# Planned landing times of GpSimd's small loads in an encoder trunk whose instruction order is planned

## The chip, the core and the metric

The kernel runs on one core of one Trainium2 chip. The metric is the device time of one execution in microseconds (us). TensorE does the matrix products (the profile calls it PE, and its weight loads PEld), VectorE (DVE) and ScalarE (ACT) prepare operands and evaluate results, GpSimd (POOL) does small vector work and issues a part of the DMA transfers, and SyncE (SP) issues the rest. Each engine works through its own instructions strictly in the order in which they stand in its queue; semaphores order the engines against each other.

## What is computed

Two layers of a macaron encoder on 256 tokens of width 1024, in float32:

```
for l in range(2):
    x = LN(alpha*x + 0.5*swiglu(x, ffn_w_in[l,0], ffn_w_out[l,0]))   # D_FF = 2816
    y = mlstm(x) if l == 0 else window_attention(x)
    x = LN(alpha*x + y)
    x = LN(alpha*x + 0.5*swiglu(x, ffn_w_in[l,1], ffn_w_out[l,1]))
```

The mLSTM projects x to q, k, v (4 heads), an output gate, and 16 gate columns (input and forget gates of both directions). From the gates it forms per head and direction a running sum and a running maximum over the tokens; the weights `exp(u - max)` multiply the products q k, and the result multiplies v.

## The kernel before

**How the work is tiled.** The weights stream from HBM in words of 128 x 1024 numbers (512 KB, one DMA each). A word is split into two float32r parts: ACT casts it to `w_hi`, DVE subtracts to get `w_lo`, and PE multiplies three times (hi by hi, hi by lo, lo by hi) with moving operands 512 wide. There are ten buffers for `w_hi` and ten for `w_lo`, so ACT and DVE can run ten words ahead of PE; raw words and other tiles of that size share sixteen buffers called "big". The feed-forward layers use a seven-product scheme for blocks of 512 columns (products P1, P2, S1 to S4, A22), in which some words are sums of two blocks: either DVE adds them, or POOL issues a DMA that adds a block from HBM onto the word in place (tiles `b11`, `b12`, `b22`). Between the products stand transposes of the finished activations (T0, T1) and one word each of the second matrix (`d`). `h_hi` and `h_lo` are the split transposed activations; their PSUM bank is free again when DVE has written `h_lo`.

**What sets the order.** The kernel body does not issue instructions. Each call is noted as a `Step` with its operands in a `Book`, and the order is planned afterwards. `latest` (line 392) gives each step a due time: PE's steps follow each other in program order, and every other step is due its own duration (and the delay until its result is seen) before the earliest step that needs it. `sequence` (line 420) then plays the engines against modelled durations: at each point it takes the step that can start first, and among those that can start the one that is due first; PE keeps program order. The steps are emitted in the order that comes out (line 596, which is therefore the line of nearly every instruction in the profile), and a step's buffer is chosen on the way. So a number in the model does not act on the chip by itself; it moves instructions within the queues of DVE, ACT, POOL and SP, and it can change which buffer a tile gets.

**The small loads.** A constant tile `few` of 128 x 192 holds small things that POOL loads with its own DMAs (`small_loads`, line 723, noted at the end of the first feed-forward stage): `gw`, the 16 gate columns of the mLSTM's input matrix (64 KB in runs of 64 bytes, since each of the 1024 matrix rows gives 16 numbers), four pieces of four gate biases (after a memset), the norm gains, and the attention sinks, which POOL then negates. ACT casts the gate columns to the float32r tile that is also named `gw` (after POOL has cleared it), and DVE writes its low part. Near the end of the gate arithmetic, POOL issues two DMAs that copy the running maximum from the tile `scan` into a tile `most`, one row per head (line 1242); `partition_broadcast` on POOL (line 1267, "ISA" in the order, PARTITION_BROADCAST in the profile) spreads each row over all partitions into the tiles `wt`, one per head; ACT takes exponentials of them, POOL masks them with `affine_select`, and `scores` (line 1294) and `mix` (line 1310) use them.

**What the planner thought of these DMAs.** Line 417 puts a plain DMA's due time LANDING + LOADING, that is 2200 + 1400 ns, ahead of its first reader, and line 519 lets data of a plain DMA on POOL land the same 3600 ns after its issue. DMAs that add (`accum_op`) and the loads on SP have their own rules.

Of the kernel before, what the change touches and what calls it, by code (L numbers as in the profile page):

```python
# [58 lines left out]
ISSUE = 600.0  # L59
LANDING = 2200.0  # L60
LOADING = 1400.0
ADDING = 5500.0
QUEUED = 6000.0
RING = {"SP": (2000.0, 1250.0), "POOL": (2900.0, 1150.0)}
# [186 lines left out]
class Book:  # L251
# [140 lines left out]
    def latest(self):  # L392
        steps = self.steps
        extra = [[] for _ in steps]
        for kind, rooms in self.rooms.items():
            held, free = [], HOMES[kind][1]
            for r in rooms:
                if free:
                    free -= 1
                else:  # L400
                    held.sort(key=lambda x: x.last)
                    old = held.pop(0)
                    assert old.last < r.first, ("no room", kind, r.name, [x.name for x in held])
                    for s in old.steps:
                        extra[s.n].append(r.first)
                held.append(r)
        t = 0.0
        for s in steps:
            if s.engine == "PE":
                s.due = t  # L410
                t += s.takes
        for s in reversed(steps):
            if s.engine == "PE":
                continue
            after = s.later + s.takes
            if s.name == "dma_start":
                after += ADDING + LANDING if s.kw.get("accum_op") is not None else LANDING + LOADING
            s.due = min([steps[d].due for d in [*s.succ, *extra[s.n]]], default=t + 5000.0) - after

    def sequence(self):  # L420
# [54 lines left out]
        while len(given) < len(steps):  # L475
            best = None
            for e, list_ in todo.items():
# [7 lines left out]
                for n in cands:  # L485
                    s = steps[n]
# [21 lines left out]
            s = steps[n]  # L508
# [7 lines left out]
            s.lands = s.end + s.later  # L516
            if s.name == "dma_start":
                if e == "POOL" and s.kw.get("accum_op") is None:
                    s.lands = s.end + LANDING + LOADING
                elif loads < len(RAMP):  # L520
                    dma = s.lands = RAMP[loads]
                    rings.t = dma - RING[e][1]
                    loads += 1
                else:
                    for n_, t_ in rings.add(s).items():
                        steps[n_].lands = t_ + SPARE[steps[n_].engine]
                        if steps[n_].engine == "SP":
                            dma = max(dma, t_) if n_ == n else dma
                    loads += 1
# [1084 lines left out]
```

## Time and profile before

| | us |
|---|---|
| median of 3 runs | 911.31 (909.03 to 912.22) |
| the profiled execution, its own time | 910.23 |
| its span in the trace | 908.5 |
| PE busy | 894.7 |
| DVE busy | 815.5 |
| ACT busy | 635.6 |
| POOL busy | 156.8 |
| mean granted clock of TensorE | 0.995 |

Times in the views count from the start of the span. A timeline row has the start, the length, the engine, the line, the operation with the tile that it writes and the tiles that it reads, and in brackets the idle time of the engine before it with what ended it. The chain of waits follows the work that ended last back to the start: where a DMA stands in it, that transfer was what the next engine waited for. A row of the windows view gives a stretch, its length, busy time and number of instructions of PE, PEld, DVE, ACT and POOL, then the granted clock of TensorE, the DMA share and GB/s.

### The profile page before, as it was taken

The numbers are of one execution on the slowest core, as the hardware profiler recorded it, in microseconds if no ns is written. First come the engines' busy times: TensorE is split into PE (matmuls) and PEld (weight loads), VectorE is DVE, ScalarE is ACT, GpSimd is POOL, SyncE is SP. The second block draws the span as 40 slices with busy tenths as digits, with TensorE's granted clock in tenths as the row PEclk, the third lists the DMA queues.
The fourth block names the chain that finished last, engine by engine and source line by source line (L and its number), as shares of the span: only waits on it lengthen the run. The fifth ranks groups of instructions, "written<-read, shape, count | busy, mean of one in ns | idle before, by whom it ended". The sixth has DMA issues, their size and how long they took to land.

```text
span 908.5 us, 12627 instructions
## 1 busy us (share of the span) xinstructions
PE 894.7 (98%) x4387; PEld 747.2 (82%) x4387; DVE 815.5 (90%) x1008; ACT 635.6 (70%) x881; POOL 156.8 (17%) x194
## 2 busy tenths in 40 slices
PE   9999998999999999999999999999999999999996
PEld 7888886888988888888888888888898788888885
DVE  7999987678797999999879999997789999999975
ACT  6777666557754887776768767775688887777650
POOL 0121221013111212122021211130134221212200
PEclk9999998999999999999999999999999999999999
DMA  9999996943386889999985899999542778999931
GB/s 317 381 302 266 275 318 172 356 141 116 119 256 158 213 233 327 265 274 295 334 258 141 223 321 298 269 255 371 186 119 78 223 167 236 326 266 281 285 83 46
DMA packets 106111, 216.92 MB, mean 239 GB/s; under 512 B 7192, under 2 KB 23600, under 8 KB 106048
## 3 DMA queue, kind: packets, MB, share of 16 engines
q1 hardware_dynamic: 84000, 174.09, 54.0%
q0 software_dynamic: 22048, 42.04, 26.9%
q8 instruction: 34, 0.56, 0.2%
q14 instruction: 29, 0.24, 0.1%
HBM read 215.04 MB, written 1.05 MB: 238 GB/s over the span
## 4 chain that ended last, share of the span: by engine, by line
PE 86%; DVE 8%; issue 2%; ACT 2%; DMA 1%; DVEq 0%; POOL 0%; ACTq 0%
PE pw L596 54%; PE py L596 32%; DVE w_lo L596 4%; DVE b L596 1%; DMA few<-in_ml_w_in_dram 1%; ACT w_hi L596 1%; DVE x L596 1%; DVE e L596 0%; DVE S L596 0%; DVE pr L596 0%; DMA x<-in_x_dram 0%; DVE pv L596 0%; DVE h_lo L596 0%; ACT xT_hi L596 0%; DVE few L596 0%
## 5 line engine op out<-in xcount | busy, mean ns | idle before, releaser
L596 ACT CAST w_hi<-b 128x1024 fp32r<-128x1024 f32 x266 | 277.7, 1053 | 98.8 <-PE py L596 54.0
L596 DVE TENSOR_TENSOR w_lo<-b,w_hi 128x1024 fp32r<-128x1024 f32 x266 | 317.4, 1219 | 14.5 <-ACT w_hi L596 14.5
L596 DVE TENSOR_TENSOR w_lo<-raw,w_hi 128x1024 fp32r<-128x1024 f32 (+1 forms) x158 | 187.2, 1207 | 11.3 <-ACT w_hi L596 9.8
L596 PE MATMUL pw<-w_hi,S 128*128 128x512 f32 x608 | 195.1, 390 | 0.3 <-DVE h_lo L596 0.3
L596 ACT CAST w_hi<-raw 128x1024 fp32r<-128x1024 f32 (+1 forms) x158 | 162.9, 1042 | 37.5 <-PE pw L596 19.4
L596 POOL DMA_DIRECT2D b<-in_ffn_w_in_dram x80 | 96.9, 1216 | 493.8 <-DVE b L596 188.6
L596 PE MATMUL pw<-w_hi,xT_hi 128*128 128x512 f32 (+1 forms) x420 | 165.8, 396 | 4.2 <-DVE h_lo L596 4.0
L596 PE MATMUL pw<-w_hi,xT_lo 128*128 128x512 f32 (+1 forms) x420 | 163.6, 391 | 0.0
L596 PE MATMUL pw<-w_lo,xT_hi 128*128 128x512 f32 (+1 forms) x420 | 162.0, 389 | 0.0
L596 PEld LDWEIGHTS pw<-w_hi,S 128*128 128x128 f32 x608 | 114.1, 188 | 25.0 <-DVE h_lo L596 1.2
L596 PE MATMUL py<-w_hi,h_hi 128*128 128x512 f32 x317 | 125.6, 396 | 0.0
L596 PE MATMUL py<-w_hi,h_lo 128*128 128x512 f32 x317 | 123.8, 391 | 0.0
L596 PE MATMUL py<-w_lo,h_hi 128*128 128x512 f32 x317 | 123.4, 389 | 0.0
L596 PE MATMUL pw<-w_lo,S 128*128 128x512 f32 x304 | 118.3, 389 | 0.0
L596 PEld LDWEIGHTS pw<-w_hi,xT_hi 128*128 128x128 f32 x420 | 79.6, 190 | 20.1 <-DVE h_lo L596 4.4
L596 PEld LDWEIGHTS pw<-w_hi,xT_lo 128*128 128x128 f32 x420 | 79.7, 190 | 18.6 <-DVE xT_lo L596 2.1
L596 PEld LDWEIGHTS pw<-w_lo,xT_hi 128*128 128x128 f32 x420 | 79.4, 190 | 14.8
L596 DVE TENSOR_TENSOR b<-b,b 128x1024 f32<-128x1024 f32 x72 | 87.7, 1220 | 0.8
L596 PEld LDWEIGHTS py<-w_hi,h_lo 128*128 128x128 f32 x317 | 59.5, 188 | 12.9 <-DVE h_lo L596 0.3
L596 PEld LDWEIGHTS py<-w_lo,h_hi 128*128 128x128 f32 x317 | 59.7, 188 | 11.8
L596 PEld LDWEIGHTS py<-w_hi,h_hi 128*128 128x128 f32 x317 | 59.7, 188 | 11.7
L596 PEld LDWEIGHTS pw<-w_lo,S 128*128 128x128 f32 x304 | 57.1, 188 | 11.6
(205 smaller groups left out, 1103.8 us busy)
## 6 DMA issues: line engine op xcount, KB each, us to landing
b<-in_ffn_w_in_dram SPq DMA_DIRECT2D x152, 512.0 KB, 8.1
raw<-in_ffn_w_out_dram SPq DMA_DIRECT2D x88, 512.0 KB, 8.2
b<-in_ffn_w_in_dram POOLq DMA_DIRECT2D x80, 512.0 KB, 9.0
raw<-in_ml_w_in_dram SPq DMA_DIRECT2D x24, 512.0 KB, 5.5
raw<-in_ffn_w_in_dram SPq DMA_DIRECT2D x36, 256.0 KB, 6.2
raw<-in_at_w_in_dram SPq DMA_DIRECT2D x12, 512.0 KB, 9.0
raw<-in_ml_w_out_dram SPq DMA_DIRECT2D x8, 512.0 KB, 4.2
raw<-in_at_w_out_dram SPq DMA_DIRECT2D x8, 512.0 KB, 8.4
```

The source lines that it names most:

```text
L596: getattr(engines[s.engine], s.name)(*[real(x) for x in s.args], **{k: real(x) for k, x in s.kw.items()})
```

## The change

The two planned delays of 3600 ns are replaced, for plain DMAs on POOL, by a table with one entry for the copies into `most` (6600 ns) and one for the loads into `few` (9500 ns). No instruction is added, removed or given another operand; the whole order is planned again with these numbers.

```
+FEW = {"most": 6600.0, "few": 9500.0}
...
-                after += ADDING + LANDING if s.kw.get("accum_op") is not None else LANDING + LOADING
+                after += ADDING + LANDING if s.kw.get("accum_op") is not None else FEW[s.outs[0].room.name] if s.engine == "POOL" else LANDING + LOADING
...
                 if e == "POOL" and s.kw.get("accum_op") is None:
-                    s.lands = s.end + LANDING + LOADING
+                    s.lands = s.end + FEW[s.outs[0].room.name]
```

PE's order is the same in both kernels, row for row, and so is SP's. What moves stands on POOL, ACT and DVE. In the changed kernel all lines behind the table have a number that is one higher (L597 for L596).

The first place is POOL's queue in the last third of the first feed-forward stage. `b12_1018` and `b12_1096` are words onto which POOL's DMA adds a block, `few_74` is the tile of small things, and `gw_1259` (`gw_1261` after) the cleared tile for the gate columns. Before:

```order
L596 DMA b11_739<-in_ffn_w_in_dram 128x2x512
L596 MEMSET few_74 128x2
L596 DMA b12_1018<-in_ffn_w_in_dram 128x2x512
L596 DMA b12_1096<-in_ffn_w_in_dram 128x2x512
L596 DMA few_74<-in_ml_w_in_dram 128x8x16
L596 MEMSET few_74 128x1
L596 DMA few_74<-in_ml_gate_b_dram 4x1
L596 MEMSET gw_1259 128x1024
L596 DMA few_74<-in_ml_gate_b_dram 4x1 x3
L596 DMA b11_929<-in_ffn_w_in_dram 128x2x512
```

and now:

```order
L597 DMA b11_739<-in_ffn_w_in_dram 128x2x512
L597 MEMSET few_74 128x2
L597 MEMSET few_74 128x1
L597 DMA few_74<-in_ml_gate_b_dram 4x1
L597 DMA few_74<-in_ml_w_in_dram 128x8x16
L597 DMA few_74<-in_ml_gate_b_dram 4x1
L597 DMA b12_1018<-in_ffn_w_in_dram 128x2x512
L597 DMA b12_1096<-in_ffn_w_in_dram 128x2x512
L597 DMA few_74<-in_ml_gate_b_dram 4x1
L597 MEMSET gw_1261 128x1024
L597 DMA few_74<-in_ml_gate_b_dram 4x1
L597 DMA b11_929<-in_ffn_w_in_dram 128x2x512
```

The load of the gate columns, the bias memset and two bias loads now stand ahead of the two adding DMAs instead of behind them; ACT's cast of the gate columns and PE's rows around it keep their places.

The second place is POOL's queue in the mLSTM, from the first broadcast to the last mask. `wt_1974`, `wt_1987`, `wt_2029`, `wt_2193` before and `wt_2004`, `wt_2020`, `wt_2137`, `wt_2208` after are the weights of heads 0 to 3; an ISA row is a broadcast. Before:

```order
L596 ISA wt_1974<-most_1923 128x256
L596 ISA wt_1987<-most_1923 128x256
L596 ISA wt_1974<-most_1923 128x256
L596 ISA wt_1987<-most_1923 128x256
L596 ISA wt_2029<-most_1923 128x256 x2
L596 AFFINE_SELECT wt_1974<-wt_1974 128x256 x2
L596 AFFINE_SELECT wt_1987<-wt_1987 128x256 x2
L596 AFFINE_SELECT wt_2029<-wt_2029 128x256 x2
L596 ISA wt_2193<-most_1923 128x256 x2
L596 AFFINE_SELECT wt_2193<-wt_2193 128x256 x2
```

and now, from the fourth broadcast on:

```order
L597 AFFINE_SELECT wt_2004<-wt_2004 128x256 x2
L597 ISA wt_2020<-most_1923 128x256
L597 AFFINE_SELECT wt_2020<-wt_2020 128x256
L597 ISA wt_2137<-most_1923 128x256
L597 AFFINE_SELECT wt_2020<-wt_2020 128x256
L597 ISA wt_2137<-most_1923 128x256
L597 AFFINE_SELECT wt_2137<-wt_2137 128x256
L597 ISA wt_2208<-most_1923 128x256
L597 AFFINE_SELECT wt_2137<-wt_2137 128x256
L597 ISA wt_2208<-most_1923 128x256
L597 AFFINE_SELECT wt_2208<-wt_2208 128x256 x2
```

Broadcasts and masks alternate, where before six broadcasts stood ahead of the first mask; a mask waits for ACT's exponentials of the same half of a head.

The third place is ACT's queue in the same stretch. `w_hi` rows are casts of weight words, `q_hi` and `k_hi` evaluations of the projections, and ACTIVATE `wt` the exponentials (three per half of a head). Before:

```order
L596 CAST w_hi_2010<-raw_1725 128x1024
L596 ACTIVATE wt_1974<-wt_1974,ucol_2017 128x128 x3
L596 CAST q_hi_2039<-pw_1957 128x512
L596 ACTIVATE wt_1974<-wt_1974,ucol_2017 128x128 x3
L596 ACTIVATE wt_1987<-wt_1987,ucol_2017 128x128 x6
L596 ACTIVATE wt_2029<-wt_2029,ucol_2017 128x128 x6
L596 CAST w_hi_2107<-raw_1740 128x1024
```

and now, the last part, ahead of the cast of head 0's weights:

```order
L597 ACTIVATE wt_2208<-wt_2208,ucol_2013 128x128 x3
L597 ACTIVATE w_hi_2242<-raw_2085,few_74 128x1024
L597 ACTIVATE wt_2208<-wt_2208,ucol_2013 128x128 x2
L597 ACTIVATE k_hi_2196<-pw_2183 128x512
L597 ACTIVATE wt_2208<-wt_2208,ucol_2013 128x128
L597 ACT_TABLE_LOAD
L597 ACTIVATE w_hi_2281<-raw_2105,few_74 128x1024
L597 ACTIVATE w_hi_2291<-raw_2126,few_74 128x1024
L597 CAST a_hi_2304<-wt_2004 128x768
```

Eighteen exponentials stood nearly in one piece before; now they are spread between casts of weight words, and the last of them, the table load behind it and two casts stand directly ahead of `a_hi` of head 0. The rest of the change is small: the load of the attention sinks stands one row earlier on POOL, and on DVE some steps of the mLSTM's four heads swap places with each other and with `w_lo` rows.

## The prediction

> **What bounds the kernel now.** I read the page's busy times first, then who PE waits for, then PE's timeline around its longest wait, and last the chain of waits behind it.
>
> ```profile
> span 908.5 us, 12627 instructions
> PE 894.7 (98%) x4387; PEld 747.2 (82%) x4387; DVE 815.5 (90%) x1008; ACT 635.6 (70%) x881; POOL 156.8 (17%) x194
> PE pw L596 <- DVE h_lo L596: 4.2, 2, 4.0
> PE py L596 <- DVE zero L596: 1.2, 1, 1.2
> ```
>
> PE is busy for all but 13.8 us of its span. Whatever the change does on other engines counts only where it ends or starts a wait of PE, and in the middle of the run there is one of size: 4.0 us behind DVE's `h_lo`; the next in the list, 1.2 us, is the start of the run. PE's timeline shows it, between the transposes T0 and T1 of a column block in the first feed-forward stage; the last two rows are the same pair of transposes in the second feed-forward stage.
>
> ```profile
> 134.98 0.60 PE L596 MATMUL pw<-ident,e 128*128 128x128 f32 x4
> ...
> 142.30 0.80 PE L596 MATMUL pw<-w_hi,xT_hi 128*128 128x512 f32 x1 [3.97 <-DVE h_lo L596]
> ...
> 150.41 0.60 PE L596 MATMUL pw<-ident,e 128*128 128x128 f32 x4
> ...
> 391.10 0.60 PE L596 MATMUL pw<-ident,e 128*128 128x128 f32 x4
> ...
> 399.75 0.60 PE L596 MATMUL pw<-ident,e 128*128 128x128 f32 x4
> ```
>
> From T0 to T1 stand the same 24 matmuls in both places. They take 399.75 - 391.10 = 8.65 us undisturbed, and 150.41 - 134.98 = 15.43 us here: 6.78 us are lost. Of these 3.97 are the wait; the other 2.81 follow it, because PE then runs at a lower clock, as the windows view shows (the last three numbers are the granted clock, the DMA share and GB/s):
>
> ```profile
> 140.00:144.00 4.00, 1.70 (x4) 1.41 (x5) 3.79 (x5) 2.87 (x5) 0.00 (x0) 0.62 0.00 0
> ```
>
> The Trainium skill ("TensorE: Matmul & The Clock Gate", Part 1) says that after an idle window PE runs at half clock until about 3.4 us of activity have passed; an estimate from that page is 1.7 us lost after the wait, 5.7 in all, and a time of 905.6. This trace has 2.81, and it decides.
>
> The chain of waits and ACT's timeline tell why `h_lo` was late.
>
> ```profile
> 125.22 1.24 DVE b L596
> ...
> 127.47 10.41 DMA few<-in_ml_w_in_dram
> ...
> 141.56 0.69 DVE h_lo L596
> ```
>
> ```profile
> 129.78 1.06 ACT L596 CAST w_hi<-b 128x1024 fp32r<-128x1024 f32 x1 [0.35 <-PE pw L596]
> 137.96 0.57 ACT L596 CAST gw<-few 128x32 fp32r<-128x32 f32 x4 [7.13 <-DMA few<-in_ml_w_in_dram]
> ```
>
> ACT comes to the cast of the gate columns at 130.84 and waits 7.13 us for a load that PE needs only in the next stage. Two weight casts, the activation `g` and `h_hi` stand behind it on ACT, `h_lo` behind `h_hi` on DVE, and PE's next product needs the bank that `h_lo` frees.
>
> **Step 1: the gate columns.** POOL's timeline shows where the load can go now.
>
> ```profile
> 109.42 1.20 POOL L596 DMA_DIRECT2D b<-in_ffn_w_in_dram  x1 [10.89 <-DVE w_lo L596]
> 111.69 1.20 POOL L596 DMA_DIRECT2D b<-in_ffn_w_in_dram  x1 [1.06 <-DVE w_lo L596]
> 112.42 0.59 POOL L596 MEMSET few<- 128x2 f32 x1
> 124.58 1.21 POOL L596 DMA_DIRECT2D b<-in_ffn_w_in_dram  x1 [11.57 <-PE py L596]
> 126.74 1.20 POOL L596 DMA_DIRECT2D b<-in_ffn_w_in_dram  x1 [0.96 <-DVE b L596]
> 127.47 1.42 POOL L596 DMA_DIRECT2D few<-in_ml_w_in_dram  x1
> 129.30 0.60 POOL L596 DMA_DIRECT2D few<-in_ml_gate_b_dram  x1 [0.30 <-POOL few L596]
> 130.51 0.96 POOL L596 MEMSET gw<- 128x1024 f32 x1 [0.61 <-DVE w_lo L596]
> ```
>
> POOL sat idle for 11.57 us ahead of the adding DMA at 124.58. The bias memset, one bias load, the gate columns and another bias load (0.59 + 0.30 + 0.60 + 1.42 + 0.60 = 3.5 us) fit in from 113.0 to 116.5, 8 us before that DMA can go, so nothing that is pushed back is late. The gate columns are issued near 114.5. With the same 10.41 us they land at 124.9, 5.9 us before ACT asks. ACT's cast also needs POOL's clearing of the tile, which waited for DVE at 130.51 and still does: it ends at 131.47, so ACT keeps a wait of 0.6 us of its 7.13.
>
> What is late next? After the cast (0.57) two weight casts follow; `g` can start only when PE has finished the product before T0, at about 135.1 (T0's first matmul stands at 134.98). From there it is DVE that decides:
>
> ```profile
> 134.08 1.23 DVE L596 TENSOR_TENSOR b<-b,b 128x1024 f32<-128x1024 f32 x1
> 139.51 1.22 DVE L596 TENSOR_TENSOR w_lo<-b,w_hi 128x1024 fp32r<-128x1024 f32 x1 [4.21 <-ACT w_hi L596]
> 140.95 0.69 DVE L596 TENSOR_TENSOR e<-g,e 128x512 f32<-128x512 f32 x1 [0.21 <-ACT g L596]
> ```
>
> The sum at 134.08 ends at 135.31; then `w_lo` 1.22, `e` 0.69 and `h_lo` 0.69 without a wait give 137.9. PE would come to its product at 142.30 - 3.97 = 138.33. That is 0.4 us of room, so I take the whole wait as gone, and the low clock with it: 6.8 us, with 0 to 1 us of the wait left as the unkind bound. It cannot gain much beyond that, as the list has no further wait of PE of any size.
>
> Behind that point ACT runs ten words ahead of PE again, as it did before (its row at 129.78 waited for PE, not for data). The load itself moves into a stretch in which SP issues weight loads (the second row has their size and the time from issue to landing).
>
> ```profile
> 112.61 2.93 SPq L596 DMA_DIRECT2D b<-in_ffn_w_in_dram  x3
> b<-in_ffn_w_in_dram SPq DMA_DIRECT2D x3, 512.0 KB, 8.8
> ```
>
> They take 8.8 us. The first of them, half of the word that DVE adds at 125.22, lands near 121.4, 3.8 us early. The 64 KB are an eighth of one such load; even at twice that share of 8.8 us, an estimate of 2.2 us, the delay is covered. I take nothing.
>
> **Step 2: the copies into `most`.** PE never waits in the mLSTM, so nothing can be gained there, only lost.
>
> ```profile
> L596 POOL PARTITION_BROADCAST wt<-most x8: 547/548/2964, 220.4 to 229.5; - x8
> L596 POOL TENSOR_SCALAR_AFFINE_SELECT wt<-wt x8: 406/406/417, 226.0 to 237.0; 128x256 f32<-128x256 f32 x8
> 222.17 2.96 POOL L596 PARTITION_BROADCAST wt<-most  x1
> 222.37 2.35 DVE L596 TENSOR_TENSOR w_lo<-raw,w_hi 128x1024 fp32r<-128x1024 f32 x2
> 236.59 0.39 ACT L596 ACTIVATE wt<-wt,ucol 128x128 f32<-128x128 f32 x1
> 237.00 1.28 ACT L596 ACT_TABLE_LOAD   x1
> 238.29 2.31 ACT L596 ACTIVATE w_hi<-raw,few 128x1024 fp32r<-128x1024 f32 x2
> 244.20 0.84 ACT L596 CAST a_hi<-wt 128x768 fp32r<-128x768 f32 x1 [0.74 <-DVE wt L596]
> 245.22 0.95 DVE L596 TENSOR_TENSOR a_lo<-wt,a_hi 128x768 fp32r<-128x768 f32 x1
> 246.53 0.29 PE L596 MATMUL py<-v_hi,a_lo 128*128 128x258 f32 x1
> ```
>
> The tight place is head 0: `a_lo` is ready at 246.17 and PE uses it at 246.53, 0.36 us later. Before, the table load and the first two scaled casts were done at 240.60. Now the last exponential, the table load and two scaled casts stand between the last broadcast and `a_hi`: 0.39 + 1.28 + 2.31 = 3.98 us. PE starts to wait when the last broadcast ends after 244.20 - 3.98 + 0.36 = 240.6. I count it: start 220.4 (the first one's), eight broadcasts, six masks between them at 0.41 (2.4) and five hand-overs to ACT for three exponentials at 0.39 (5.9). With six broadcasts at the median 0.55 and two that DVE holds up, at 2.96, they take 9.2 and the last ends at 237.9, 2.7 us early. So the mLSTM costs nothing. The bounds are 0 and, with half of the eight held up (four at 2.96 and four at 0.55, 14.0 in all), an end at 242.7 and a wait of 2.1 us.
>
> The later heads have no such edge: the last mask of the trace before ended at 237.0 + 0.4, and head 3's weights are cast at
>
> ```profile
> 259.34 0.84 ACT L596 CAST a_hi<-wt 128x768 fp32r<-128x768 f32 x1 [0.57 <-DVE wt L596]
> ```
>
> 20 us later.
>
> **Step 3: the sinks.** Their load moves one row up, ahead of
>
> ```profile
> 595.34 1.20 POOL L596 DMA_DIRECT2D b<-in_ffn_w_in_dram  x1 [2.63 <-ACT w_hi L596]
> ```
>
> POOL was idle for 2.63 us there, and the issue takes at most the 1.42 of the gate columns: nothing.
>
> **The sum.** 910.23 - 6.8 = 903.4 for the profiled execution, whose span is 908.5 with 1.7 us around it. The median of the runs lies 1.1 us above that execution, and the changed kernel will be measured by a median too, so I predict 911.3 - 6.8 = 904.5.
>
> **The rivals.** *Something of the wait stays* (0.13): the 0.4 us of room on DVE is not there, because the sum at 134.08 or the clearing of the tile comes later. PE then waits 1 to 3 us and may lose some clock: 904.5 + 1 to 3.5, say 907. For it speaks that the room is small; against it, that every link stands in a row with its duration.
>
> *The change does not do what it says* (0.05): the gate columns land late again. They stand now behind two adding DMAs issued at 109.4 and 111.7 instead of behind two others. They would have to take from 114.5 to beyond 137, 22 us instead of 10.4: 911.
>
> *The broadcasts decide* (0.05), and the kernel becomes slower. The place is the alternation of broadcasts and masks, which spreads the broadcasts over the time in which DVE writes `w_lo` row after row: the broadcast at 222.17 took 2.96 us beside two of these, against 0.55 at the median. The Trainium skill ("GPSIMD Engine Reference", section 1, Specifications) states that POOL shares its SBUF interfaces with VectorE and contends with instructions of two SBUF inputs; by that, as the trace agrees, each broadcast beside a `w_lo` would be slow. With all eight at 2.96 (23.7) the last ends at 220.4 + 23.7 + 8.3 = 252.4, PE waits 11.8 us and loses another 2.8 at low clock: 904.5 + 14.6 = 919. The points from which it decides: PE begins to wait at 1.5 us per broadcast ((240.6 - 220.4 - 8.3) / 8), the gain is eaten at 2.0 (a wait of 4.0 and 2.8 of low clock), and from 2.3 on the kernel is slower by over 0.3%. Against it speaks that ACT's exponentials wait for the broadcasts and the casts behind them feed DVE: a late broadcast makes DVE idle, and then goes through.
>
> **How the numbers follow.** The forecast has 0.74, the rivals 0.13, 0.05 and 0.05; 0.03 I leave to what I have not seen, such as a load that now gets another buffer. The forecast's own spread is that of the runs, 909.0 to 912.2 less 6.8: 902.2 to 905.4. The range takes in the rest of a wait and the mLSTM's bound: 902.2 to 908.0. A measurement of this kernel can tell about 0.3%, 2.7 us, from no change, so "faster" means below 908.6: forecast, most of the first rival and of the rest, 0.88; within 0.3% 0.07; slower 0.05.
>
> **What would show it right or wrong.** Right: ACT waits under 1 us ahead of `gw`, PE has no wait on `h_lo` near 138 us, T0 to T1 takes about 8.7 us, and in the mLSTM PE's stretches from 200 to 280 us are full, 6.8 us earlier in all. Wrong: PE waits for ACT or DVE at head 0's `a_hi` or `a_lo`, broadcasts of 2 us and more, or the load of the gate columns landing after ACT has come to it.

## The result, and the profile after

The changed kernel takes 903.33 us (median of 4 runs, 902.68 to 903.97) against 910.88 for the kernel before (4 runs, 909.03 to 912.22): a ratio of 0.9918, 95% interval 0.9899 to 0.9938. In a second comparison, with five new runs of it beside 19 of before, it was 904.39 against 910.47, ratio 0.9931, interval 0.9918 to 0.9943. The profiled execution of the changed kernel took 903.97 us, 6.26 less than that of before.

The page and the list of what PE waits for:

```profile
span 902.3 us, 12624 instructions
PE 891.5 (99%) x4387; PEld 744.5 (83%) x4387; DVE 815.5 (90%) x1008; ACT 635.5 (70%) x881; POOL 158.1 (18%) x194
```

```profile
PE py L597 <- DVE zero L597: 1.2, 1, 1.2
PE pw L597 <- DVE h_lo L597: 0.9, 1, 0.9
PE pw L597 <- DVE pr L597: 0.4, 1, 0.4
```

The 4.0 us behind `h_lo` are gone. The 0.9 us that the list shows under the same name stand elsewhere, in the second feed-forward stage. PE's timeline of the changed kernel has T0, T1 and that wait:

```profile
134.61 0.60 PE L597 MATMUL pw<-ident,e 128*128 128x128 f32 x4
143.25 0.60 PE L597 MATMUL pw<-ident,e 128*128 128x128 f32 x4
...
365.28 0.50 PE L597 MATMUL pw<-w_hi,S 128*128 128x512 f32 x1 [0.89 <-DVE h_lo L597]
```

T0 to T1 takes 8.64 us instead of 15.43. POOL, ACT and DVE of the changed kernel show each link of step 1:

```profile
113.57 0.99 POOL L597 DMA_DIRECT2D few<-in_ml_w_in_dram  x1
...
124.21 1.24 POOL L597 DMA_DIRECT2D b<-in_ffn_w_in_dram  x1 [9.14 <-PE py L597]
...
130.12 0.95 POOL L597 MEMSET gw<- 128x1024 f32 x1 [1.99 <-DVE w_lo L597]
```

```profile
few<-in_ml_w_in_dram POOLq DMA_DIRECT2D x1, 64.0 KB, 7.9
```

```profile
131.11 0.58 ACT L597 CAST gw<-few 128x32 fp32r<-128x32 f32 x4 [0.65 <-POOL gw L597]
...
134.81 0.60 ACT L597 ACTIVATE g<-pw 128x512 f32<-128x512 f32 x1 [0.31 <-PE pw L597]
```

```profile
133.70 1.23 DVE L597 TENSOR_TENSOR b<-b,b 128x1024 f32<-128x1024 f32 x1
...
136.58 0.68 DVE L597 TENSOR_TENSOR h_lo<-pw,h_hi 128x512 fp32r<-128x512 f32 x1
```

The load is issued at 113.57 and takes 7.9 us; ACT's cast waits 0.65 us, and what it waits for is now POOL's clearing of the tile, no longer the load. `h_lo` ends at 137.26. PE never stops: the windows view, which showed a clock of 0.62 here, has

```profile
140.00:144.00 4.00, 4.00 (x22) 3.32 (x21) 4.00 (x5) 2.58 (x4) 2.43 (x3) 1.00 0.57 120
160.00:360.00 200.00, 200.00 (x1062) 171.57 (x1061) 169.38 (x238) 136.71 (x210) 35.72 (x43) 1.00 0.71 211
```

and in the second row PE is full through the mLSTM. The broadcasts of the changed kernel:

```profile
L597 POOL PARTITION_BROADCAST wt<-most x8: 544/548/1432, 213.4 to 229.6; - x8
```

None takes 2.96 us any more, and the last ends near 230.1.

From T0 to the last transposes (890.86 before, 884.58 now) the two traces differ as follows: 6.79 us gained between T0 and T1; 0.61 lost from the transposes at 330.13 to those at 384.46 (54.33 us, against 53.72 from 337.38 to 391.10 before); 0.39 lost from 761.95 to 784.58 (22.63 against 22.24). The rest adds up to 0.12 gained.

### The profile page after: what moved, and what is told of

Same layout as the page of the kernel before. It is cut to its first block, busy times and chain, and to the rows that moved or that the text cites. A ratio compares the mean times of both kernels' runs of the same rounds, so it can differ in the third digit from the quotient of the medians.

```text
span 902.3 us, 12624 instructions
## 1 busy us (share of the span) xinstructions
PE 891.5 (99%) x4387; PEld 744.5 (83%) x4387; DVE 815.5 (90%) x1008; ACT 635.5 (70%) x881; POOL 158.1 (18%) x194
## 4 chain that ended last, share of the span: by engine, by line
PE 90%; DVE 5%; DMA 2%; ACT 2%; issue 1%; SPq 0%; DVEq 0%; ACTq 0%; POOLq 0%
PE pw L597 56%; PE py L597 33%; DVE w_lo L597 2%; DMA b<-in_ffn_w_in_dram 1%; ACT w_hi L597 1%; DVE b L597 1%; DMA raw<-in_ffn_w_in_dram 1%; DVE e L597 0%; DVE pr L597 0%; DVE x L597 0%; DVE pv L597 0%; DVE few L597 0%; ACT S L597 0%; DVE sc L597 0%; SPq L597 0%
## 5 line engine op out<-in xcount | busy, mean ns | idle before, releaser
L597 ACT CAST w_hi<-b 128x1024 fp32r<-128x1024 f32 x266 | 277.5, 1053 | 102.1 <-PE py L597 47.5
L597 DVE TENSOR_TENSOR w_lo<-b,w_hi 128x1024 fp32r<-128x1024 f32 x266 | 317.0, 1217 | 9.1 <-ACT w_hi L597 8.8
L597 DVE TENSOR_TENSOR w_lo<-raw,w_hi 128x1024 fp32r<-128x1024 f32 (+1 forms) x158 | 187.6, 1205 | 11.0 <-ACT w_hi L597 9.4
L597 PE MATMUL pw<-w_hi,S 128*128 128x512 f32 x608 | 195.1, 390 | 0.9 <-DVE h_lo L597 0.9
L597 ACT CAST w_hi<-raw 128x1024 fp32r<-128x1024 f32 (+1 forms) x158 | 163.1, 1042 | 40.2 <-PE pw L597 21.7
L597 POOL DMA_DIRECT2D b<-in_ffn_w_in_dram x80 | 97.0, 1217 | 489.3 <-DVE b L597 183.9
L597 PE MATMUL pw<-w_hi,xT_hi 128*128 128x512 f32 (+1 forms) x420 | 164.3, 393 | 0.6 <-DVE xT_hi L597 0.2
L597 PE MATMUL pw<-w_hi,xT_lo 128*128 128x512 f32 (+1 forms) x420 | 162.2, 388 | 0.2 <-DVE xT_lo L597 0.2
L597 PE MATMUL pw<-w_lo,xT_hi 128*128 128x512 f32 (+1 forms) x420 | 161.2, 386 | 0.0
L597 PEld LDWEIGHTS pw<-w_hi,S 128*128 128x128 f32 x608 | 114.1, 188 | 25.7 <-DVE h_lo L597 1.8
L597 PE MATMUL py<-w_hi,h_hi 128*128 128x512 f32 x317 | 125.5, 396 | 0.0
L597 PE MATMUL py<-w_hi,h_lo 128*128 128x512 f32 x317 | 123.7, 390 | 0.0
L597 PE MATMUL py<-w_lo,h_hi 128*128 128x512 f32 x317 | 123.4, 389 | 0.0
L597 PE MATMUL pw<-w_lo,S 128*128 128x512 f32 x304 | 118.5, 390 | 0.0
L597 PEld LDWEIGHTS pw<-w_hi,xT_lo 128*128 128x128 f32 x420 | 78.8, 188 | 18.3 <-DVE xT_lo L597 2.2
L597 PEld LDWEIGHTS pw<-w_hi,xT_hi 128*128 128x128 f32 x420 | 78.8, 188 | 16.2 <-ACT xT_hi L597 0.8
L597 PEld LDWEIGHTS pw<-w_lo,xT_hi 128*128 128x128 f32 x420 | 78.8, 188 | 15.0 <-DVE w_lo L597 0.4
L597 DVE TENSOR_TENSOR b<-b,b 128x1024 f32<-128x1024 f32 x72 | 87.6, 1219 | 0.8
L597 PEld LDWEIGHTS py<-w_hi,h_lo 128*128 128x128 f32 x317 | 59.5, 188 | 12.7
L597 PEld LDWEIGHTS py<-w_lo,h_hi 128*128 128x128 f32 x317 | 59.6, 188 | 11.8
L597 PEld LDWEIGHTS py<-w_hi,h_hi 128*128 128x128 f32 x317 | 59.6, 188 | 11.7
L597 PEld LDWEIGHTS pw<-w_lo,S 128*128 128x128 f32 x304 | 57.1, 188 | 11.9 <-DVE w_lo L597 0.3
```

The source lines that it names most:

```text
L597: getattr(engines[s.engine], s.name)(*[real(x) for x in s.args], **{k: real(x) for k, x in s.kw.items()})
```

## The experiments

In none of them does the computation change: they move rows or issue a row several times.

**Each half alone.** `few_alone` has only the delay of the loads into `few`, `most_alone` only that of the copies:

```
-FEW = {"most": 6600.0, "few": 9500.0}
+FEW = {"most": 3600.0, "few": 9500.0}
```

and, for the second,

```
-FEW = {"most": 6600.0, "few": 9500.0}
+FEW = {"most": 6600.0, "few": 3600.0}
```

> Only the delay of the loads into few is new (9500 ns); the copies into most keep 3600, so ACT's and DVE's orders are those of before and only POOL's early part and the row of the sinks change. Theory (the gate columns' load is the whole gain): T0 to T1 takes 8.6 to 8.7 us, no PE wait on h_lo near 138 us, time 903.3 or less. If the 0.55 us that the changed kernel loses again in the second feed-forward stage comes from the new mLSTM order, this kernel does not lose it: 902.8. Rival (the mLSTM's new order carries part of the gain): 905 or more.

> Only the copies into most are planned later (6600 ns); the loads into few keep 3600, so the mLSTM's order is the new one and the gate columns' load stays where it was before. Theory (the gate columns are the whole gain): PE waits 4.0 us behind h_lo near 142 us as before, T0 to T1 15.4 us, time 910.9, within 1 us of before. Rival (the mLSTM's order carries part of it): 909 or less. Rival (the spread broadcasts cost, hidden in the changed kernel): 912 or more.

`few_alone`: 904.92 us against 911.03, ratio 0.9931 (0.9915 to 0.9947), T0 to T1 8.64. `most_alone`: 910.06 against 911.03, ratio 0.999 (0.998 to 1.000). The gain is that of the loads into `few`, and the mLSTM's order is worth at most 1 us, which these runs hardly tell from nothing. The time of `few_alone` is 1.6 us above the 903.3 that was expected, close to the 905 of its rival, but `most_alone` does not come near the 909 that the same rival asks for. What was expected of the 0.55 us fell as well: PE's timeline of `few_alone`, which has the mLSTM order of before, shows the loss in the second stage all the same, and a larger one (55.18 us from 330.00 to 385.18):

```profile
366.00 0.50 PE L597 MATMUL pw<-w_hi,S 128*128 128x512 f32 x1 [1.15 <-DVE h_lo L597]
```

PE's timeline of `most_alone` holds something that no expectation had:

```profile
135.81 0.60 PE L597 MATMUL pw<-ident,e 128*128 128x128 f32 x4
143.14 0.57 PE L597 MATMUL pw<-w_hi,xT_hi 128*128 128x512 f32 x1 [3.99 <-DVE h_lo L597]
150.32 0.60 PE L597 MATMUL pw<-ident,e 128*128 128x128 f32 x4
```

The wait is that of before (3.99 against 3.97), but T0 to T1 takes 14.51 us instead of 15.43: only 1.88 us are lost beside the wait, not 2.81.

**Two other ways to take the wait away.** `one_row` moves the gate columns' load alone, past one adding DMA (against the changed kernel's table):

```
-FEW = {"most": 6600.0, "few": 9500.0}
+FEW = {"most": 3600.0, "few": 4500.0}
```

> Before, with the gate columns' load moved one row up on POOL, ahead of the second of the two adding DMAs, and no other row moved on any engine (few 4500 ns, most 3600 ns). It is issued near 125.3 instead of 127.47. If its 10.41 us are its own, it lands at 135.7, ACT is held 4.9 us, PE waits 1.8 us behind h_lo and loses 1 to 2 us more at a low clock: 907 to 908. If they are mostly the second adding DMA's, which the load then no longer follows, it lands near 133, ACT's cast is over before the activation g can start, and PE does not wait at all: 904. Theory: the first, since the load also follows the adding DMA of 124.58.

904.02 us against 911.03, ratio 0.992 (0.9904 to 0.9936). ACT's timeline and the DMA issues of `one_row`:

```profile
133.58 0.58 ACT L597 CAST gw<-few 128x32 fp32r<-128x32 f32 x4 [1.71 <-DMA few<-in_ml_w_in_dram]
```

```profile
few<-in_ml_w_in_dram POOLq DMA_DIRECT2D x1, 64.0 KB, 7.2
```

The first theory fell. The load is issued at 126.34, 9.67 us ahead of T0 (136.01 in this run), where before it was 7.51 (127.47 and 134.98): 2.16 us earlier. It takes 7.2 us instead of 10.4 now that it no longer follows the second adding DMA on POOL's queue, so one row on POOL is worth 5.4 us of landing. ACT is held for 1.71 us, less than the 3.16 that it had to spare before, and PE does not wait there.

`cast_later` leaves the load where it was and moves ACT's cast; on POOL two of the bias loads and the scaling of the sinks move back with it. Against before, in `sequence`:

```
-                    s.lands = s.end + LANDING + LOADING
+                    s.lands = s.end + (9500.0 if s.outs[0].room.name == "few" else LANDING + LOADING)
```

> The load of the gate columns stays behind both adding DMAs, as before; only ACT's cast of it is planned later, behind h_hi and one weight cast (five rows down). Theory (the wait counts only because h_hi and the product of 142 us stand behind ACT's cast): ACT comes to the cast near 137.0, waits about 1 us, nothing that PE needs soon stands behind it, T0 to T1 takes 8.6 to 8.8 us, time 903.5 to 904.5, the same gain without moving the load. Rival (the late load itself disturbs PE, by its transfer or by POOL's queue): 908 or more.

903.53 us against 911.03, ratio 0.9917 (0.99 to 0.9933), T0 to T1 8.64. ACT's timeline of `cast_later`:

```profile
136.13 0.60 ACT L596 ACTIVATE g<-pw 128x512 f32<-128x512 f32 x1 [0.26 <-PE pw L596]
136.62 0.58 ACT L596 CAST h_hi<-pw 128x512 fp32r<-128x512 f32 x1
137.09 1.06 ACT L596 CAST w_hi<-b 128x1024 fp32r<-128x1024 f32 x1
139.10 0.67 ACT L596 CAST gw<-few 128x32 fp32r<-128x32 f32 x4 [0.95 <-DMA few<-in_ml_w_in_dram]
```

The load takes 10.6 us and is as late as before, and the whole gain is there: what cost was never the transfer, but the place of the waiting row in ACT's queue, ahead of `g` and `h_hi`.

**The wait put back, in doses.** The changed kernel with POOL clearing the tile of the gate columns five, six or eight times, so that ACT's cast waits although the load has long landed (in `emit`, six shown):

```
-            getattr(engines[s.engine], s.name)(*[real(x) for x in s.args], **{k: real(x) for k, x in s.kw.items()})
+            for _ in range(6 if s.name == "memset" and s.outs[0].room.name == "gw" else 1):
+                getattr(engines[s.engine], s.name)(*[real(x) for x in s.args], **{k: real(x) for k, x in s.kw.items()})
```

> The changed kernel, with POOL clearing the tile of the gate columns six times instead of once; nothing else moves. ACT's cast then waits for POOL: 0.65 + 5 x 0.9 to 0.96 = 5.2 to 5.5 us, a wait put back in place of the one that the change removed, but shorter (7.13 before). Of 7.13 us ACT had 3.16 to spare (PE waited 3.97), so PE should wait 2.0 to 2.3 us behind h_lo. Theory (the low clock costs in proportion, 2.81 for 3.97): another 1.4 to 1.6 us, T0 to T1 12.1 to 12.5 us, time 906.8 to 907.2. Rival (a wait of 2 us leaves the clock at 1.00, as the waits of 0.9 to 1.2 us near 365 do): T0 to T1 10.6 to 10.9 us, time 905.3 to 905.6. The Trainium skill (TensorE: Matmul & The Clock Gate, Part 1) speaks for the rival: it gives an idle window of about 3.4 us before the clock drops. Rival to both (the wait at h_lo did not come from ACT's cast): 903.3.

> As clear_six with five clearings of the tile: six took 6.02 us, about 1.01 each, and held ACT for 5.72, so five hold it for 4.7 and PE waits 4.7 - 3.15 = 1.55 us behind h_lo near 140. Theory (the low clock comes in whole stretches of about 3.4 us and costs about 1.9 each, whatever the length of the wait, once a wait is long enough): either nothing is added, T0 to T1 10.2, or 1.9 is, T0 to T1 12.1; nothing in between. Rival (it costs in proportion, 0.7 per us of wait): 1.1 is added, T0 to T1 11.3.

> As clear_six with eight clearings: ACT is held for 7.7 us and PE waits 4.6 us, longer than before's 3.97. Theory (whole stretches of about 3.4 us): 1.9 us more for one stretch or 2.8 to 3.4 for two, T0 to T1 15.1 or 16.0 to 16.6. Rival (in proportion): 3.3 more, T0 to T1 16.5. That the load has long landed and the same time is lost shows that it was ACT's wait that cost, not the load's transfer: time 909 to 911, all of the gain gone.

and the kernel before, unchanged, profiled again:

> The kernel before once more, for a second profile of its wait: 910.9. The wait behind h_lo is 3.97 us again, since it is made of the load's 10.4 us. What follows it is open: 2.81 us were lost at a low clock in its first profile, 1.87 in the profile of most_alone, whose wait is the same 3.99. If the size follows from the order, it is 2.8 again; if it depends on where the wait falls among the clock's stretches, it is 1.9 or 2.8 as it comes.

`clear_five` takes 905.97 us (ratio to before 0.9955, 0.994 to 0.997), `clear_six` 907.88 (0.9969, 0.9958 to 0.998), `clear_eight` 910.48 (1.0001, 0.9987 to 1.0015), `before_again` 911.23 (1.0012, 1.0000 to 1.0023). With eight clearings all of the gain is gone again. PE's timeline has the wait of each (five, six, eight, and before again):

```profile
140.73 0.50 PE L598 MATMUL pw<-w_hi,xT_hi 128*128 128x512 f32 x1 [1.56 <-DVE h_lo L598]
```

```profile
140.51 0.77 PE L598 MATMUL pw<-w_hi,xT_hi 128*128 128x512 f32 x1 [2.57 <-DVE h_lo L598]
```

```profile
142.25 0.79 PE L598 MATMUL pw<-w_hi,xT_hi 128*128 128x512 f32 x1 [4.58 <-DVE h_lo L598]
```

```profile
142.20 0.79 PE L596 MATMUL pw<-w_hi,xT_hi 128*128 128x512 f32 x1 [4.38 <-DVE h_lo L596]
```

The clock after them is read from windows of 1 us (the number after the five engines is the granted clock). `clear_six`:

```profile
140.00:141.00 1.00, 0.49 (x1) 0.47 (x2) 1.00 (x2) 0.55 (x1) 0.00 (x0) 0.79 0.00 0
...
143.00:144.00 1.00, 1.00 (x3) 0.77 (x3) 1.00 (x2) 0.56 (x1) 0.98 (x1) 0.51 0.00 0
144.00:145.00 1.00, 1.00 (x6) 0.79 (x5) 1.00 (x2) 0.49 (x1) 0.30 (x1) 1.00 0.07 8
```

and before:

```profile
140.00:141.00 1.00, 0.00 (x0) 0.00 (x0) 0.79 (x2) 1.00 (x3) 0.00 (x0) 0.98 0.00 0
141.00:142.00 1.00, 0.00 (x0) 0.00 (x0) 1.00 (x2) 1.00 (x2) 0.00 (x0) 0.50 0.00 0
...
147.00:148.00 1.00, 1.00 (x4) 0.77 (x4) 0.92 (x1) 0.17 (x1) 0.91 (x2) 0.61 0.61 156
```

and `most_alone`, with the wait of before:

```profile
143.00:144.00 1.00, 0.86 (x3) 0.69 (x4) 1.00 (x2) 0.18 (x1) 0.00 (x0) 0.72 0.00 0
...
146.00:147.00 1.00, 1.00 (x4) 0.76 (x3) 1.00 (x2) 0.93 (x1) 0.91 (x1) 0.57 0.00 0
```

A mean between 1.00 and 0.50 tells how much of the window was low: 0.79 is 0.42 us, 0.51 is 0.98, so the clock of `clear_six` was at half from 140.58 to 143.98, 3.40 us. In before it was from 140.96 to 147.78, 6.82 us, in `most_alone` from 143.44 to 146.86, 3.42 us. The same reading for all of them, with ACT's wait ahead of its cast of the gate columns, and the moment at which the clock fell against the end of PE's wait:

| kernel | ACT's wait, us | PE's wait, us | the clock fell | half clock | T0 to T1, us | lost beside the wait (less 8.64 and the wait) |
|---|---|---|---|---|---|---|
| `clear_five` | 4.71 | 1.56 | not at all | none | 10.49 | 0.29 |
| `clear_six` | 5.72 | 2.57 | 0.07 us after it | 3.40 us | 13.11 | 1.90 |
| `most_alone` | 7.14 | 3.99 | 0.30 us after it | 3.42 us | 14.51 | 1.88 |
| before | 7.13 | 3.97 | 1.34 us ahead of it | 6.82 us | 15.43 | 2.82 |
| `before_again` | 7.54 | 4.38 | 0.70 us ahead of it | 6.82 us | 16.16 | 3.14 |
| `clear_eight` | 7.74 | 4.58 | 0.99 us ahead of it | 6.84 us | 16.26 | 3.04 |

PE's wait is ACT's less 3.15 or 3.16 us in all six, whether the load or POOL's clearing holds ACT. In `before_again` the load took 10.8 us, so its wait is not the 3.97 that was expected.

Both of the theories of `clear_six` were off: its 1.90 fit the proportional one by chance, and 3.99 us with the same 1.88 show that there is no proportion. The low clock comes in stretches of 3.4 us, one or two. In these executions it is one where PE is at work again when the clock falls, and two where PE still waits; so two equal waits (3.97 and 3.99) can draw a different number. When it falls does not follow the wait either: in the five with a low clock it falls next at the end of the run, 757.68 to 757.76 us after it rose, which is 222 stretches of 3.413 us in each; in `broadcasts_thrice`, below, it is 658.76 us, 193 stretches. This is read from few executions, and none was made to test it.

`clear_five` comes out near "nothing is added", and PE's rows show its 0.29 us:

```profile
138.79 0.39 PE L598 MATMUL py<-w_hi,h_lo 128*128 128x512 f32 x1
...
141.07 0.40 PE L598 MATMUL pw<-w_lo,xT_hi 128*128 128x512 f32 x1
```

Undisturbed, each row of 0.39 us is followed by the next 0.227 us after its start (137.80 to 143.01 in the changed kernel, 23 steps). The product after the wait starts 1.94 us after the row at 138.79, 1.56 of which are the wait and 0.16 the lost overlap, and the next row starts 0.34 us after it, 0.11 more than undisturbed. At half clock the rows stand 0.427 us apart (142.89 to 147.16 in before, ten steps), so a microsecond of work at half clock loses 0.47. The half clocks of the table, less what PE still waited in them, are 3.40, 3.42, 5.48, 6.12 and 5.85 us; 0.29 us plus 0.47 of each make 1.88, 1.89, 2.85, 3.15 and 3.03 us, and 1.90, 1.88, 2.82, 3.14 and 3.04 were lost.

**Broadcasts that cost three times as much** (the same line of `emit`, in the changed kernel).

```
+            for _ in range(3 if s.name == "partition_broadcast" else 1):
```

> The changed kernel, with each of the eight broadcasts issued three times in its place on POOL; no other row moves. The eight take 5.4 us now (0.67 each), and three times as much is 16.1 (2.0 each), the price at which the rival of the prediction counted the gain as eaten: PE waits 4 us at head 0 and loses 2.8 at low clock, 910. The prediction's own count, from the first broadcast at 213.45: 16.1 + 2.4 for six masks + 5.9 for the hand-overs ends at 237.9, 4.5 us after the 233.4 from which PE waits (240.6 less 7.2), which is the same: 908 to 910. If POOL's idle time between the broadcasts takes up the rest (it waits 1.3 to 3.6 us for ACT four times), the wait is under 1 us: 903.3 to 904.5.

910.06 us against 910.47, ratio 0.999 (0.9981 to 0.9999): the gain is eaten. The eight triples take 19.3 us, 2.4 each. But the place is another than the rival named. PE's and ACT's timelines of `broadcasts_thrice`:

```profile
228.75 0.35 PE L598 MATMUL pw<-xT_hi,w_hi 128*128 128x256 f32 x1 [1.05 <-DVE q_lo L598]
235.62 0.47 PE L598 MATMUL pw<-w_hi,xT_hi 128*128 128x512 f32 x1 [0.88 <-DVE k_lo L598]
240.97 0.39 PE L598 MATMUL pw<-q_hi,k_hi 128*128 128x256 f32 x1 [2.35 <-DVE k_lo L598]
```

```profile
230.22 0.99 ACT L598 ACTIVATE wt<-wt,ucol 128x128 f32<-128x128 f32 x3 [2.13 <-POOL wt L598]
231.12 1.98 ACT L598 CAST w_hi<-raw 128x1024 fp32r<-128x1024 f32 x2
233.01 0.58 ACT L598 ACTIVATE k_hi<-pw 128x512 fp32r<-128x512 f32 x1
```

ACT stands at the exponentials until a broadcast comes, with weight casts and `q_hi` or `k_hi` queued behind them; it is the same trap as that of the gate columns. Head 0's `a_hi` and `a_lo` are not waited for. The mLSTM's stretch, from the transposes that follow T1 to those that follow the mLSTM, grows from 151.37 (`after_again`) to 157.93 us, 6.56, of which 4.28 are the three waits. The clock was at half for 3.42 us after the last of them (241.84 to 245.26), 1.6 us at the price above; three new starts of PE can make up most of the other 0.7. So the 910 that was expected came, but by another way.

**The changed kernel again, and the two halves that did best.** `cast_and_most` plans the copies as the changed kernel does and moves ACT's cast instead of the load (in `latest`):

```
-                after += ADDING + LANDING if s.kw.get("accum_op") is not None else FEW[s.outs[0].room.name] if s.engine == "POOL" else LANDING + LOADING
+                after += ADDING + LANDING if s.kw.get("accum_op") is not None else LANDING + LOADING
```

> The changed kernel itself, on the same chip as the other three of this group: 903.3, within 1 us. It is here for two questions. The second feed-forward stage, from the transposes at 330.13 to those at 384.46, took 54.33 us in its first profile and 53.44 to 55.18 in the others: if that follows from the order, it is 54.3 again, with a wait of 0.9 us behind h_lo near 365; if it follows from how long an adding DMA happens to take, it can come out anywhere from 53.4 to 55.2. The first stage does not change: T0 to T1 8.64 us.

> The copies into most planned later as in the changed kernel, and ACT's cast of the gate columns planned later instead of their load earlier: the two halves that did best so far. Theory (the first stage is cured either way, and the mLSTM's order is worth nothing to PE): the same as the changed kernel on this chip within 0.5 us, T0 to T1 8.6 us. If the 1.0 us by which the late copies alone were better than before is theirs, it is below cast_later's 903.5: 902.5 to 903.

`after_again` takes 904.39 us, `cast_and_most` 904.36 (ratio to before 0.9928, 0.9914 to 0.9943): the same, and no version beats the changed kernel. The second feed-forward stage of `after_again` takes 53.42 us where the same kernel took 54.33 before, and has no wait behind `h_lo`:

```profile
330.64 0.60 PE L597 MATMUL pw<-ident,e 128*128 128x128 f32 x4
...
384.06 0.60 PE L597 MATMUL pw<-ident,e 128*128 128x128 f32 x4
```

The DMA issues of one adding DMA and of the SP load beside it, issued between 323.5 and 326, in the first profile of the changed kernel and in `after_again`:

```profile
b<-in_ffn_w_in_dram POOLq DMA_DIRECT2D x1, 512.0 KB, 9.7
raw<-in_ffn_w_out_dram SPq DMA_DIRECT2D x1, 512.0 KB, 7.3
```

```profile
b<-in_ffn_w_in_dram POOLq DMA_DIRECT2D x1, 512.0 KB, 7.6
raw<-in_ffn_w_out_dram SPq DMA_DIRECT2D x1, 512.0 KB, 4.2
```

The same program, the same place, and 2 to 3 us between the two executions. The loss in the second stage is not made by the order: it comes and goes with the time of the adding DMA. In the thirteen profiles of this document it took 7.5 to 8.9 us in the eight whose second stage takes 53.42 to 53.72 us, and 9.7, 10.1, 10.4, 10.5 and 10.5 in the other five, with 54.33, 54.70, 55.06, 55.11 and 55.18 us; both groups hold kernels with the old and with the new mLSTM order. Why it takes longer in one execution than in the next stays open. Nor is `after_again` free of such losses: its third feed-forward stage has 23.74 us (504.21 to 527.95) where the first profile has 22.25 (504.62 to 526.87).

## Why the prediction was right

The forecast was 904.5 us, and 903.33 and 904.39 were measured. How close it came is in part luck: it starts from a median of three runs (911.31; 910.88 with a fourth, 910.47 in the second comparison) and takes off a low clock of 2.81 us that is one draw of several.

*Step 1* went as worked out. The load was issued at 113.57 (forecast near 114.5) and landed at 121.5, 9 us before ACT came, ACT's remaining wait is 0.65 us and ends with POOL's clearing (0.6), `h_lo` left PE 0.54 us of room (137.26 to PE's product at 137.80; 0.4 was forecast), and T0 to T1 takes 8.64 us (8.7). Two numbers were off without harm. The load took 7.9 us, not 10.41; `one_row` shows that 3.2 of the 10.4 belonged to the adding DMA directly ahead of it on the queue, so the price of a load is that of its place. And from T0 to T1 stand 36 matmuls of 512 columns behind the four transposes, not 24; they are the same in both places, so 8.65 us is the right measure. `cast_later` and `clear_eight` settle that ACT's row was the cause: the first has the whole gain with the load as late as before, the second has none of it with the load as early as in the changed kernel.

*The term of the sum that was mis-sized* is the low clock, 2.81 of the 6.8 us. It was read as the cost of a wait of 4 us; it is what one execution drew, 0.29 us for the new start and 0.47 of the 5.48 us that PE worked at half clock, and the others with waits of 3.99 to 4.58 us lost 1.88 to 3.14. So the gain is 5.9 (`most_alone`) to 7.5 us (`before_again`) in one execution, and the medians gave 7.55 in one comparison and 6.08 in the other. The prediction let the trace's 2.81 decide against the estimate of 1.7 from the Trainium skill ("TensorE: Matmul & The Clock Gate", Part 1). Both are right in part: `clear_six` and `most_alone`, with a half clock of 3.40 and 3.42 us, lost 1.90 and 1.88, which is one such stretch of about 3.4 us; before, `before_again` and `clear_eight` had two. The idle window of about 3.4 us that the Trainium skill (same part) puts ahead of the drop does not agree: here 2.57 us of waiting were enough (`clear_six`), and 1.56 were not (`clear_five`).

*Step 2* was right in that the mLSTM lost nothing. The last broadcast ended at 230.1, or 237.3 on before's clock (7.16 later), where 237.9 was counted, but that is luck: the eight broadcasts took 5.4 us and not the 9.2 counted, the masks and the waits for ACT 11.3 and not 8.3. Only one was slow, 1.43 us at 220.60 beside the `w_lo` of 220.40; the last three ran while DVE had none, as the prediction argued against its rival. T1 to the transposes that follow the mLSTM (331.44 and 324.20) takes 180.95 us, 181.03 before. *Step 3* cost nothing.

*The sum* was 910.23 - 6.8 = 903.43 for the profiled execution, which took 903.97. Of the 0.54 between them 0.51 are the two later stages: 0.61 and 0.39 lost there, less 0.37 by which T0 itself came earlier and 0.12 elsewhere. For the loss in the second stage the prediction had left 0.03 to a load that gets another buffer. That is not it: `few_alone` and `one_row`, with the mLSTM order of before and the same buffers for SP's loads as before, lose more in that stage, and `after_again`, with the changed ones, loses nothing there.

*The rivals.* Nothing of the wait stayed. The broadcasts did not decide. `broadcasts_thrice` gives that rival a price: its formula for 2.4 us each gives a last broadcast at 220.4 + 19.3 + 8.3 = 248.0, a wait of 7.4 us and 10.2 with the clock; 6.56 were lost. It had the danger right and the place wrong, since ACT's queue stops PE at `q_lo` and `k_lo` before head 0 is reached.

## What to carry to other kernels

When an engine that works in order stands at a row for a late transfer, look first at which rows behind it are urgent: moving the waiting row down (903.53 us) was worth as much as bringing the transfer forward (903.33), and moving a load past one adding DMA on its queue (904.02) nearly as much. Price a stall of TensorE of 2.4 us and more as its wait plus 1.9 to 3.1 us (one or two stretches of low clock), and not from a single profile, where two equal waits differed by 0.9 us. Before a small loss in a later stage is blamed on the new order, profile the same kernel twice.

## What the runs showed of the hardware

TensorE's granted clock went to one half after waits of 2.35 us (the last of the three in `broadcasts_thrice`) and more, and not after waits of 0.89 to 1.56 us; between 1.56 and 2.35 no run has a wait. It stayed there for 3.40 to 3.42 or 6.82 to 6.84 us, nothing between, and a microsecond of PE's work in it cost 0.47 us. It fell between 2.6 us (`clear_six`, whose wait began at 137.94) and 4.3 us (`most_alone`: 139.15 to 143.44) after the wait began, in the latter when the wait was already over. A 64 KB load on POOL's queue took 10.4 to 10.8 us where two adding DMAs of 512 KB had been issued 0.7 and 2.9 us ahead of it, 7.2 directly behind one, and 7.8 to 8.2 where two had been issued 2.25 and 4.5 us ahead of it. A row of three broadcasts for one takes 1.82 to 3.32 us in `broadcasts_thrice`, where nine in a row take 7.81.
